# Shift blocks of a modulated norm divided over three engines, in a two-layer decoder trunk

## The chip, the core and the metric

The kernel runs on one core of one Trainium2 chip. The metric is the device time of one execution in microseconds (us). Each engine of the core takes its own instructions in order, and they signal one another by semaphores: TensorE (PE; its weight loads are PEld) multiplies matrices, VectorE (DVE), ScalarE (ACT) and GpSimd (POOL) work elementwise, and SyncE (SP) issues nearly all DMAs.

## The reference, cut to what matters

Layer 0 is attention and a SwiGLU, layer 1 a gated short convolution and a SwiGLU. Each of the four sub-layers begins with the same modulated norm:

```
S, D = 256, 1024                       # positions, features; x, c and all weights float32
sc = silu(c)
mod = sc @ w_ada[i] + b_ada[i]         # 6 * D columns: shift, scale, gate of both sub-layers
sh_m, sc_m, g_m, sh_f, sc_f, g_f = split(mod, 6)
h = x * rsqrt(mean(x * x) + EPS) * gain * (1 + sc_m) + sh_m
...
qkv = h @ w_qkv                        # layer 0
x = x + g_m * (attention(qkv) @ w_o)
h = modulate(x, norm_ffn, sh_f, sc_f)
x = x + g_f * swiglu(h, w_gate_up, w_down)
```

The change lies mostly in layer 0's first norm: its shift `sh_m` and scale `sc_m` are sums over 1024 inputs each, and the products for q and k cannot begin without them.

## The kernel before, in words

**Layout.** Everything is kept feature by position: `xT` is 128 x 8 x 256, eight blocks of 128 features (k = 0 to 7) by 256 positions. Every float32 product is done as three with operands split in a high and a low part: ACT copies the high part (`wh`, `m0h`), DVE subtracts it (`wl`, `m0l`), and `mm3` (L254, L255, L258) issues three matmuls. With weights on the left the second and third need `m0l` and `wl`.

**Stage 1, written out by hand (L554 to L629).** PE, DVE and ACT run exactly the order of the code. A prologue transposes x on PE (`turn_x`), sums its squares, and makes the row factors `rows0`. Then the loop runs over the eight feature blocks k: PE does block k's 36 matmuls into six accumulators (four `pq`, two `pk`), while the other engines make the operands of block n = k + 1:

- `scale_column` (L494): DVE sums the scale of block n over 1024 inputs (L109, one multiplication with a running sum) and turns it into one column (L492).
- `w_part` (L509): ACT copies and DVE subtracts the weights `wf_qk`, in three parts; the first before the norm's steps, two behind them.
- `normed` (L499): DVE multiplies the x block by its scale column and by `rows0`, into `t`.
- `h_operand` (L504): ACT adds the shift, into `m0h`; DVE makes `m0l` from `t`, the shift and `m0h`.
- The shift: `mod_sums` (L463) sums it on PE in the middle of block k's matmuls, ACT copies the result out (L473), `mod_columns` (L476) turns it to a column on PE, and ACT adds the bias (L487). For n = 1 this is one block; for n = 2, 4, 6 it covers blocks n and n + 1 together (256 columns wide).

`ja, jb` say behind which of the six accumulators the sums and the columns stand. `keep_warm` issues idle matmuls in the prologue. DVE is thus asked, for each block, for a sum, a column, a part of `wl`, `t`, `m0l`, and two parts of `wl`, in that order.

**Loads.** SP issues all loads in program order into five buffers of 1 MB (tag `wf`); a load waits until the buffer's last reader is done. A `wa_sh` buffer holds the shift matrices of two blocks, a `wa_sc` buffer the scale matrices of two.

**The rest** is ordered by a scheduler. `raw_gemm` (L414) begins the next three sub-layers: it multiplies weights by x before the norm is known, 12 matmuls per block k, and squeezes between them `norm.rstd()` (L347: PE sums the squares, ACT takes the root, DVE the reciprocal) in front of k = 2, and `norm.rows()` (L359: PE turns the result) in front of k = 4.

Of the kernel before, what the change touches and what calls it, by code (L numbers as in the profile page):

```python
# [30 lines left out]


@with_exitstack
def trunk_kernel(ctx: ExitStack, tc: tile.TileContext, x_t, cols_in, scale_in, shift_in, ada_in, qk_rows, kv_in, o_in,
                 in_in, out_in, gu_in, down_in, out_f):
    nc = tc.nc

    const = ctx.enter_context(tc.tile_pool(name="const", bufs=1))
# [375 lines left out]
    def raw_gemm(keys, norm, name):  # L414


        raw = norm.raw
        pss = [[psum.tile([P, S + 2], F32, tag=tag, name=f"raw_{name}_{i}{o}", bufs=n) for o in range(2)]
               for i, (tag, n) in enumerate((("gemm", 4), ("alt", 2)))]
        ws = [get(k) for k in keys]  # L420
        for k in range(KD):
            if k == 2:
                norm.rstd()
            if k == 4:
                rows = norm.rows()
                with tc.high_priority(400):
                    hs = modulated(norm.l, norm.sh, norm.scl, rows, name)
            for ps, (wh, wl) in zip(pss, ws):
                for o in range(2):
                    cs = slice(o * P, (o + 1) * P)  # L430
                    mm3(ps[o], (wh[:, k, cs], wl[:, k, cs]), (raw[0][:, k], raw[1][:, k]), k == 0, k == KD - 1)
        settle(name)
        res = []
        for i, tag in enumerate("sa"):
            y = tmp.tile([P, 2, S], F32, tag=tag, name=f"rawy_{name}_{i}")
            b = tmp.tile([P, 2], F32, tag="rawb", name=f"rawb_{name}_{i}")
            for o in range(2):
# [38 lines left out]
    def mod_columns(y, name):  # L476

        ps = ps_misc(f"mod_c_{name}")
        n = y.shape[1] // P
        for i in range(n):  # L480
            nc.tensor.matmul(ps[:, i:i + 1], y[:, i * P:(i + 1) * P], firsts, start=True, stop=True)
        return ps[:, :n]

    def shift_columns(y, k):
        ps = mod_columns(y, f"sh{k}")
        for n in range(ps.shape[1]):
            nc.scalar.activation(mcol(0, SH_M, k + n), ps[:, n:n + 1], AF.Identity,  # L487
                                 bias=b_cols[:, SH_M * KD + k + n:][:, :1])

    def scale_of(m, k, sums):  # L490

# [6 lines left out]

    def normed(k):  # L499
        t = tmp.tile([P, S], F32, tag="t", name=f"t_m0_{k}", bufs=3)  # L500
        nc.vector.scalar_tensor_tensor(t, xT[:, k], mcol(0, SC_M, k), rows0, op0=ALU.mult, op1=ALU.mult)
        return t

    def h_operand(k, t):  # L504
# [49 lines left out]
    with tc.manual_schedule(engines={mybir.EngineType.PE, mybir.EngineType.DVE, mybir.EngineType.Activation}):  # L554
# [30 lines left out]
        rr0 = rstd_rows(rstd0, "rr_0")  # L585
        rows0 = tmp.tile([P, S], F32, tag="rrow", name="rows0", bufs=1)
        nc.scalar.activation(rows0, rr0, AF.Copy)
        x_ps = turn_x(1, ps_alt)
        ps = mod_columns(y, "sc0")
        scale_of(mcol(0, SC_M, 0), 0, ps)  # L590
        y = mod_sums(shifts[:, 0:1], "sh0")
        t = normed(0)
        nc.vector.tensor_copy(xT[:, 2:4], x_ps)
        keep_warm(2)
        ops = w_operands(0, wf)
        shift_columns(y, 0)
        x_ps = [turn_x(i, ps_alt) for i in (2, 3)]
        operands(0, t, wf, ops)
        for i in range(2):
            nc.scalar.activation(xT[:, 4 + 2 * i:6 + 2 * i], x_ps[i], AF.Copy)  # L600
        keep_warm(4)
        for k in range(KD):
            n = k + 1
            if n < KD:
                if n % 2 == 0:
                    shifts, scales = ada_first(n // 2)
                    load_first(shifts, shift_in, n)
                    load_first(shifts, shift_in, n + 1)
                elif n == 1:
                    load_first(shifts, shift_in, 1)  # L610
                load_first(scales, scale_in, n)
                wf = first_rows(n)
            ja, jb = ((2, 3), (1, 2), (1, 4), (0, 3))[min(k, 3)]
            sums = n < KD and (n == 1 or n % 2 == 0)
            first_products(k, ops, range(0, ja))
            if sums:
                y = mod_sums(shifts[:, 1:2] if n == 1 else shifts, f"sh{n}")
            if n < KD:
                scale_column(scales[:, n % 2], n)
            first_products(k, ops, range(ja, jb))  # L620
# [202 lines left out]
def _lay_out(inputs):  # L823

    import numpy as np

    a = {k: np.asarray(v) for k, v in inputs.items()}

    def feats(v):
        return v.reshape(-1, P).T  # L830

    def chunks(w):

        k, j = w.shape[0] // P, w.shape[1] // CW
        return w.reshape(k, P, j, CW).transpose(2, 1, 0, 3).reshape(j, P, k * CW)

    ada = a["w_ada"].reshape(DEPTH, D, 6, KD, P)
    turned = ada.transpose(0, 2, 3, 4, 1)
    qkv = a["w_qkv"][0]

    def sums(part):

        return ada[0, :, part].reshape(KD, P, KD, P).transpose(2, 1, 0, 3).reshape(KD, P, D)

    return {
        "x_tok": a["x"][0].reshape(2, P, D).transpose(1, 0, 2),
        "cols": np.concatenate([feats(a[n]) for n in ("b_ada", "norm_mix", "norm_ffn", "conv_w", "q_gain", "k_gain", "c")],
                               axis=1),
        "scale": np.concatenate([sums(SC_M)[:1], turned[0, SC_M, 1:]]),
        "shift": sums(SH_M),  # L850
        "ada": turned.reshape(DEPTH, 6, 4, 2, P, D).transpose(0, 1, 2, 4, 3, 5).reshape(DEPTH, 6, 4, P, 2 * D),
        "qk_rows": qkv[:, :D + D // 2].reshape(KD, P, D + D // 2),
        "kv": chunks(qkv[:, D + D // 2:]),
        "o": chunks(a["w_o"][0]),
        "in": chunks(a["w_in"][0]),
        "out": chunks(a["w_out"][0]),
        "gate_up": np.stack([chunks(w) for w in a["w_gate_up"]]),
        "down": np.stack([chunks(w) for w in a["w_down"]]),
    }
# [21 lines left out]
```

## Time and profile before

| | us |
|---|---|
| median of 3 runs (lowest to highest) | 587.23 (586.2 to 587.33) |
| the profiled execution: its time, its span | 586.6, 584.8 |
| PE busy, share of the span | 577.4, 99% |
| DVE busy, ACT busy | 454.8 (78%), 316.1 (54%) |
| GpSimd busy | 1.1 |

The 1.8 us between the profiled time and its span lie before the first and after the last instruction. "Busy" counts a matmul from its start to its modelled end, and matmuls overlap, so short waits of PE do not show in that share: they are read from the starts of neighbouring matmuls, or from a wait that is named. Stage 1 reaches from the start to about 53 us.

### The profile page before, as it was taken

What the parts mean: (1) busy time and instruction counts of PE and PEld (TensorE: products, weight loads), DVE (VectorE), ACT (ScalarE), POOL (GpSimd) and SP (SyncE); (2) the same over time, 40 slices, a digit from 0 to 9 for tenths busy, and PEclk for the clock granted to TensorE, in tenths of its full rate; (3) what the DMA queues carried; (4) which work ended last, traced back from release to release, by engine and by line L of the source; (5) the groups of instructions that cost most, each with busy time, mean ns of one, the idle gap of its engine ahead of it and who ended that gap; (6) DMA issues with size and microseconds to landing.
All of it is one profiled execution on the core that took longest, in us unless ns stands there. A gap on an engine that the chain in (4) does not pass through costs nothing.

```text
span 584.8 us, 12020 instructions
## 1 busy us (share of the span) xinstructions
PE 577.4 (99%) x5032; PEld 569.8 (97%) x5032; DVE 454.8 (78%) x722; ACT 316.1 (54%) x526; POOL 1.1 (0%) x8
## 2 busy tenths in 40 slices
PE   7999999999999999999999999999999999999997
PEld 6899999999999999999999999999999999999997
DVE  4789989999999798967977999759986576555550
ACT  6457889597644454544445745446745345443330
POOL 0000000000000000000000000000000000000000
PEclk9999999999999999999999999999999999999999
DMA  8999999955898999968986379637387566655400
GB/s 316 396 380 409 356 331 334 341 208 187 335 377 303 347 334 342 331 240 303 330 310 254 129 291 366 247 122 261 128 331 280 180 261 216 238 174 200 148 19 18
DMA packets 25109, 156.04 MB, mean 267 GB/s; under 512 B 2784, under 2 KB 3168, under 8 KB 8928
## 3 DMA queue, kind: packets, MB, share of 16 engines
q1 hardware_dynamic: 25056, 155.28, 71.8%
q8 instruction: 39, 0.64, 0.4%
q14 instruction: 14, 0.11, 0.0%
HBM read 154.22 MB, written 1.05 MB: 266 GB/s over the span
## 4 chain that ended last, share of the span: by engine, by line
PE 93%; DMA 2%; DVE 2%; ACT 1%; issue 1%; SPq 0%; ACTq 0%; DVEq 0%
PE pu L255 7%; PE pu L254 7%; PE pu L258 7%; PE op_d L255 6%; PE op_d L254 6%; PE op_d L258 6%; PE pg L254 6%; PE pg L258 6%; PE pg L255 6%; PE raw_f L254 1%; PE op_o L258 1%; PE raw_f L255 1%; PE raw_f L258 1%; PE pb L258 1%; PE pb L254 1%; PE op_o L254 1%
## 5 line engine op out<-in xcount | busy, mean ns | idle before, releaser
L109 DVE SCALAR_TENSOR_TENSOR prod<-wa,c_all 128x1024 f32<-128x1024 f32 x80 | 97.6, 1220 | 18.0 <-DMA wa<-in_ada_dram 17.2
L98 ACT ACTIVATE wh_d<-wf_d 128x1024 fp32r<-128x1024 f32 (+1 forms) x48 | 45.2, 981 | 62.6 <-issue 41.9
L99 DVE TENSOR_TENSOR wl_d<-wf_d,wh_d 128x1024 fp32r<-128x1024 f32 (+1 forms) x48 | 52.8, 1132 | 23.9 <-ACT wh_d L98 23.7
L98 ACT ACTIVATE wh_g<-wf_g 128x1024 fp32r<-128x1024 f32 x44 | 45.7, 1053 | 44.6 <-issue 44.2
L98 ACT ACTIVATE wh_u<-wf_u 128x1024 fp32r<-128x1024 f32 x44 | 44.6, 1051 | 36.1 <-issue 30.5
L99 DVE TENSOR_TENSOR wl_u<-wf_u,wh_u 128x1024 fp32r<-128x1024 f32 x44 | 52.3, 1220 | 13.6 <-ACT wh_u L98 13.3
L99 DVE TENSOR_TENSOR wl_g<-wf_g,wh_g 128x1024 fp32r<-128x1024 f32 x44 | 53.5, 1219 | 2.4 <-ACT wh_g L98 2.2
L254 PE MATMUL op_d<-a0h,wh_d 128*128 128x256 f32 x176 | 48.6, 276 | 0.0
L258 PE MATMUL op_d<-a0h,wl_d 128*128 128x256 f32 x176 | 48.6, 276 | 0.0
L255 PE MATMUL op_d<-a1l,wh_d 128*128 128x256 f32 x176 | 48.6, 276 | 0.0
L254 PE MATMUL op_d<-a1h,wh_d 128*128 128x256 f32 x176 | 48.6, 276 | 0.0
L255 PE MATMUL op_d<-a0l,wh_d 128*128 128x256 f32 x176 | 48.6, 276 | 0.0
L258 PE MATMUL op_d<-a1h,wl_d 128*128 128x256 f32 x176 | 48.6, 276 | 0.0
L254 PE MATMUL pg<-f0h,wh_g 128*128 128x256 f32 x160 | 44.5, 278 | 0.0
L258 PE MATMUL pg<-f0h,wl_g 128*128 128x256 f32 (+3 forms) x164 | 44.5, 275 | 0.0
L254 PE MATMUL pg<-f1h,wh_g 128*128 128x256 f32 x160 | 44.3, 277 | 0.0
L255 PE MATMUL pg<-f0l,wh_g 128*128 128x256 f32 x160 | 44.2, 276 | 0.0
L254 PE MATMUL pu<-f0h,wh_u 128*128 128x256 f32 x160 | 44.2, 276 | 0.0
L258 PE MATMUL pg<-f1h,wl_g 128*128 128x256 f32 x160 | 44.2, 276 | 0.0
L258 PE MATMUL pu<-f1h,wl_u 128*128 128x256 f32 x160 | 44.2, 276 | 0.0
L255 PE MATMUL pu<-f0l,wh_u 128*128 128x256 f32 x160 | 44.2, 276 | 0.0
L255 PE MATMUL pg<-f1l,wh_g 128*128 128x256 f32 x160 | 44.2, 276 | 0.0
(294 smaller groups left out, 2022.8 us busy)
## 6 DMA issues: line engine op xcount, KB each, us to landing
wa<-in_ada_dram SPq DMA_DIRECT2D x40, 1024.0 KB, 6.8
wf_g<-in_gate_up_dram SPq DMA_DIRECT2D x22, 1024.0 KB, 5.3
wf_u<-in_gate_up_dram SPq DMA_DIRECT2D x22, 1024.0 KB, 4.9
wf_d<-in_down_dram SPq DMA_DIRECT2D x16, 1024.0 KB, 6.1
wf_d<-in_down_dram SPq DMA_DIRECT2D x8, 768.0 KB, 5.3
wa_sc<-in_scale_dram SPq DMA_DIRECT2D x8, 512.0 KB, 6.9
wa_sh<-in_shift_dram SPq DMA_DIRECT2D x8, 512.0 KB, 7.9
wf_qk<-in_qk_rows_dram SPq DMA_DIRECT2D x8, 512.0 KB, 6.7
```

The lines of the kernel that those rows point to most:

```text
L98: nc.scalar.activation(wh[:, a:b], wf[:, a:b], AF.Copy)
L99: nc.vector.tensor_sub(wl[:, a:b], wf[:, a:b], wh[:, a:b].bitcast(F32))
L109: nc.vector.scalar_tensor_tensor(t, w, 1.0, c_all, op0=ALU.mult, op1=ALU.mult, accum_out=dst)
L254: nc.tensor.matmul(ps, ah, bh, start=first, stop=False, skip_group_check=True)
L255: nc.tensor.matmul(ps, ah, bl, start=False, stop=False, skip_group_check=True)
L258: nc.tensor.matmul(ps[:, a:b], al, bh[:, a:b], start=False, stop=last, skip_group_check=True)
```

## The change

Four edits, in words: (1) The shift of odd blocks (n = 1, 3, 5, 7) is no longer summed on PE: its matrix is laid out like the scale's, DVE sums it with `ada_sum` (L109), ACT adds the bias. PE's sums for n = 2, 4, 6 become 128 columns wide instead of 256. (2) GpSimd multiplies x by `rows0`, blocks 1 to 7, into a new tensor `xn`; `normed` becomes an ACT multiplication of `xn` by the scale column. (3) In the prologue, block 0's shift sum goes in front of the transposes of the second pair of x blocks, and two `keep_warm` calls go. (4) `norm.rstd()` stands in front of k = 3 instead of k = 2. The array `out` (w_out, 4 MB) becomes the first argument, in front of x, and is not used earlier than before.

```diff
@@ -152 @@ (setup)
-    room("al", 1, "first_al")
+    xn = pair_rows(room("al", KD * S, "xn"))
@@ -419 @@ raw_gemm
-            if k == 2:
+            if k == 3:
                 norm.rstd()
@@ -481 @@
+    def shift_of(k, sums):
+        nc.scalar.activation(mcol(0, SH_M, k), sums, AF.Identity, bias=b_cols[:, SH_M * KD + k:][:, :1])
@@ -498 @@ normed
-        nc.vector.scalar_tensor_tensor(t, xT[:, k], mcol(0, SC_M, k), rows0, op0=ALU.mult, op1=ALU.mult)
+        if k == 0:
+            nc.vector.scalar_tensor_tensor(t, xT[:, k], mcol(0, SC_M, k), rows0, op0=ALU.mult, op1=ALU.mult)
+        else:
+            nc.scalar.activation(t, xn[:, k], AF.Copy, scale=mcol(0, SC_M, k))
@@ -585 @@ prologue
-        x_ps = turn_x(1, ps_alt)
         ps = mod_columns(y, "sc0")
         scale_of(mcol(0, SC_M, 0), 0, ps)
         y = mod_sums(shifts[:, 0:1], "sh0")
+        x_ps = turn_x(1, ps_alt)
         t = normed(0)
         nc.vector.tensor_copy(xT[:, 2:4], x_ps)
-        keep_warm(2)
...
-        keep_warm(4)
+        for k in range(1, KD):
+            nc.gpsimd.tensor_mul(xn[:, k], xT[:, k], rows0)
@@ -611 @@ loop over k
-            sums = n < KD and (n == 1 or n % 2 == 0)
+            sums = n < KD and n % 2 == 0
             first_products(k, ops, range(0, ja))
             if sums:
-                y = mod_sums(shifts[:, 1:2] if n == 1 else shifts, f"sh{n}")
+                y = mod_sums(shifts[:, 0:1], f"sh{n}")
             if n < KD:
+                if n % 2:
+                    ada_sum(mcol(0, SH_M, n), shifts[:, 1], f"sh{n}")
                 scale_column(scales[:, n % 2], n)
             first_products(k, ops, range(ja, jb))
             if n < KD:
                 ops_n = w_operands(n, wf)
                 if sums:
                     shift_columns(y, n)
+                else:
+                    shift_of(n, mcol(0, SH_M, n))
                 t = normed(n)
@@ -845 @@ _lay_out
-        "shift": sums(SH_M),
+        "shift": np.stack([turned[0, SH_M, k] if k % 2 else sums(SH_M)[k] for k in range(KD)]),
```

DVE's order in stage 1, before, for blocks n = 3 and n = 4 (`prod_sc` is the scale sum, `wl_qk_419` and `wl_qk_483` the two blocks' low weights):

```order
L109 SCALAR_TENSOR_TENSOR prod_sc_397,mod<-wa_sc_313,c_all 128x1024
L492 SCALAR_TENSOR_TENSOR mod<-mod,b_one,cols 128x1
L512 TENSOR_TENSOR wl_qk_419<-wf_qk_388,wh_qk_418 128x512
L501 SCALAR_TENSOR_TENSOR t_m_3_422<-xT,mod,rows_185 128x256
L506 SCALAR_TENSOR_TENSOR m0l<-t_m_3_422,mod,m0h 128x256
L512 TENSOR_TENSOR wl_qk_419<-wf_qk_388,wh_qk_418 128x512 x2
L109 SCALAR_TENSOR_TENSOR prod_sc_461,mod<-wa_sc_443,c_all 128x1024
L492 SCALAR_TENSOR_TENSOR mod<-mod,b_one,cols 128x1
L512 TENSOR_TENSOR wl_qk_483<-wf_qk_447,wh_qk_482 128x512
L501 SCALAR_TENSOR_TENSOR t_m_4_491<-xT,mod,rows_185 128x256
L506 SCALAR_TENSOR_TENSOR m0l<-t_m_4_491,mod,m0h 128x256
L512 TENSOR_TENSOR wl_qk_483<-wf_qk_447,wh_qk_482 128x512 x2
```

The same place of DVE's order after the change (`prod_sh` is the new shift sum):

```order
L109 SCALAR_TENSOR_TENSOR prod_sh_383,mod<-wa_sh_300,c_all 128x1024
L109 SCALAR_TENSOR_TENSOR prod_sc_385,mod<-wa_sc_301,c_all 128x1024
L492 SCALAR_TENSOR_TENSOR mod<-mod,b_one,cols 128x1
L516 TENSOR_TENSOR wl_qk_407<-wf_qk_374,wh_qk_406 128x512
L510 SCALAR_TENSOR_TENSOR m0l<-t_m_3_411,mod,m0h 128x256
L516 TENSOR_TENSOR wl_qk_407<-wf_qk_374,wh_qk_406 128x512 x2
L109 SCALAR_TENSOR_TENSOR prod_sc_450,mod<-wa_sc_432,c_all 128x1024
L492 SCALAR_TENSOR_TENSOR mod<-mod,b_one,cols 128x1
L516 TENSOR_TENSOR wl_qk_472<-wf_qk_436,wh_qk_471 128x512
L510 SCALAR_TENSOR_TENSOR m0l<-t_m_4_478,mod,m0h 128x256
L516 TENSOR_TENSOR wl_qk_472<-wf_qk_436,wh_qk_471 128x512 x2
```

The odd block has gained a sum of 1024 elements at its head, and both blocks have lost `t_m`.

ACT's order before, from block 3's first weight part to block 4's `m0h`:

```order
L511 ACTIVATE wh_qk_418<-wf_qk_388 128x512
L505 ACTIVATE m0h<-t_m_3_422,mod 128x256
L511 ACTIVATE wh_qk_418<-wf_qk_388 128x512 x2
L473 ACTIVATE mod_y_sh_459<-mod_ps_sh_450 128x256
L511 ACTIVATE wh_qk_482<-wf_qk_447 128x512
L487 ACTIVATE mod<-mod_c_sh_486,cols 128x1 x2
L505 ACTIVATE m0h<-t_m_4_491,mod 128x256
```

The same place after the change:

```order
L515 ACTIVATE wh_qk_406<-wf_qk_374 128x512
L485 ACTIVATE mod<-mod,cols 128x1
L505 ACTIVATE t_m_3_411<-xn,mod 128x256
L509 ACTIVATE m0h<-t_m_3_411,mod 128x256
L515 ACTIVATE wh_qk_406<-wf_qk_374 128x512 x2
L473 ACTIVATE mod_y_sh_448<-mod_ps_sh_439 128x128
L515 ACTIVATE wh_qk_471<-wf_qk_436 128x512
L485 ACTIVATE mod<-mod_c_sh_475,cols 128x1
L505 ACTIVATE t_m_4_478<-xn,mod 128x256
L509 ACTIVATE m0h<-t_m_4_478,mod 128x256
```

`t_m` now stands on ACT right in front of the `m0h` that reads it.

## Rows read from the trace of the kernel before

**Rows 1.** The page: span, and busy time of each engine.
```profile
span 584.8 us, 12020 instructions
...
PE 577.4 (99%) x5032; PEld 569.8 (97%) x5032; DVE 454.8 (78%) x722; ACT 316.1 (54%) x526; POOL 1.1 (0%) x8
```

**Rows 2.** Windows: length, busy (instructions) by engine, clock, DMA share, GB/s.
```profile
26.33:48.85 22.52, 22.52 (x209) 21.10 (x208) 18.99 (x38) 10.42 (x24) 0.00 (x0) 1.00 1.02 381
```

**Rows 3.** Timeline, DVE, block 3: start, duration, instruction, [idle before it <- releaser].
```profile
26.33 1.22 DVE L109 SCALAR_TENSOR_TENSOR prod_sc<-wa_sc,c_all 128x1024 f32<-128x1024 f32 x1
...
27.59 0.22 DVE L492 SCALAR_TENSOR_TENSOR mod<-mod,b_one,cols 128x1 f32<-128x1 f32 x1
27.73 0.68 DVE L512 TENSOR_TENSOR wl_qk<-wf_qk,wh_qk 128x512 fp32r<-128x512 f32 x1
28.33 0.48 DVE L501 SCALAR_TENSOR_TENSOR t_m<-xT,mod,rows 128x256 f32<-128x256 f32 x1
29.44 0.48 DVE L506 SCALAR_TENSOR_TENSOR m0l<-t_m,mod,m0h 128x256 fp32r<-128x256 f32 x1 [0.64 <-ACT m0h L505]
...
31.17 1.22 DVE L109 SCALAR_TENSOR_TENSOR prod_sc<-wa_sc,c_all 128x1024 f32<-128x1024 f32 x1
```

**Rows 4.** Timeline, ACT: block 3's m0h, and one shift column (block 1).
```profile
16.41 0.26 ACT L487 ACTIVATE mod<-mod_c_sh,cols 128x1 f32<-128x1 f32 x1
...
28.90 0.51 ACT L505 ACTIVATE m0h<-t_m,mod 128x256 fp32r<-128x256 f32 x1 [2.77 <-DVE t_m L501]
```

**Rows 5.** Timeline, block 2: ACT's first weight part, DVE's sum and m0l.
```profile
22.21 0.63 ACT L511 ACTIVATE wh_qk<-wf_qk 128x512 fp32r<-128x512 f32 x1 [0.93 <-DMA wf_qk<-in_qk_rows_dram]
...
20.93 1.23 DVE L109 SCALAR_TENSOR_TENSOR prod_sc<-wa_sc,c_all 128x1024 f32<-128x1024 f32 x1 [1.02 <-DMA wa_sc<-in_scale_dram]
...
24.60 0.48 DVE L506 SCALAR_TENSOR_TENSOR m0l<-t_m,mod,m0h 128x256 fp32r<-128x256 f32 x1 [0.64 <-ACT m0h L505]
```

**Rows 6.** Timeline, block 7: DVE's m0l, then PE's first two matmuls.
```profile
48.85 0.48 DVE L506 SCALAR_TENSOR_TENSOR m0l<-t_m,mod,m0h 128x256 fp32r<-128x256 f32 x1 [0.64 <-ACT m0h L505]
...
49.30 0.28 PE L254 MATMUL pq<-m0h,wh_qk 128*128 128x256 f32 x1
49.42 0.36 PE L255 MATMUL pq<-m0l,wh_qk 128*128 128x256 f32 x1
```

**Rows 7.** Timeline, PE: shift sums of 128 and 256 columns, and what follows each.
```profile
14.70 0.64 PE L469 MATMUL mod_ps_sh<-wa_sh,sc 128*32 128x128 f32 x16
15.28 0.39 PE L254 MATMUL pq<-m0h,wh_qk 128*128 128x256 f32 x1
...
29.41 1.07 PE L469 MATMUL mod_ps_sh<-wa_sh,sc 128*32 128x256 f32 x16
30.41 0.38 PE L254 MATMUL pq<-m0h,wh_qk 128*128 128x256 f32 x1
```

**Rows 8.** Timeline, DVE: two sums back to back, and block 1's first instruction.
```profile
61.94 1.23 DVE L109 SCALAR_TENSOR_TENSOR prod<-wa,c_all 128x1024 f32<-128x1024 f32 x1
...
63.21 1.22 DVE L109 SCALAR_TENSOR_TENSOR prod<-wa,c_all 128x1024 f32<-128x1024 f32 x1
...
14.42 1.23 DVE L109 SCALAR_TENSOR_TENSOR prod_sc<-wa_sc,c_all 128x1024 f32<-128x1024 f32 x1
```

**Rows 9.** Timeline, GpSimd: its largest instruction that reads a tile.
```profile
1.35 0.29 POOL L77 TENSOR_SCALAR_AFFINE_SELECT causal<-causal 128x128 f32<-128x128 f32 x1
```

**Rows 10.** Timeline, PE, layer 1's convolution: the sum of squares in raw_gemm.
```profile
312.79 0.28 PE L258 MATMUL raw_m<-zvh,wl_cu 128*128 128x258 f32 x1
313.47 0.27 PE L351 MATMUL ms_n<-inv_d,ss_n 128*128 128x1 f32 x1 [0.40 <-DVE ss_n L332]
```

**Rows 11.** Timeline, DVE and PE, last raw_gemm: low weights, and the turned rows.
```profile
404.96 1.20 DVE L99 TENSOR_TENSOR wl_g<-wf_g,wh_g 128x1024 fp32r<-128x1024 f32 x1
...
406.54 0.38 PE L300 MATMUL rr_n<-ident,rs_n 128*128 128x128 f32 x2
```

**Rows 12.** DMA, 0 to 12 us: GB/s in 40 slices of 0.3 us.
```profile
GB/s 0 0 0 0 0 26 175 171 164 273 314 137 137 68 178 273 382 410 410 396 437 437 410 396 437 423 410 437 410 382 417 423 437 416 410 423 423 410 437 382
```

More of the change, by code (lines that the diff above doesn't have):

```diff
@@ L33, in trunk_kernel @@
 @with_exitstack
-def trunk_kernel(ctx: ExitStack, tc: tile.TileContext, x_t, cols_in, scale_in, shift_in, ada_in, qk_rows, kv_in, o_in,
-                 in_in, out_in, gu_in, down_in, out_f):
+def trunk_kernel(ctx: ExitStack, tc: tile.TileContext, out_in, x_t, cols_in, scale_in, shift_in, ada_in, qk_rows, kv_in,
+                 o_in, in_in, gu_in, down_in, out_f):
     nc = tc.nc
@@ L482, in mod_columns @@
         return ps[:, :n]
+    def shift_of(k, sums):
+        nc.scalar.activation(mcol(0, SH_M, k), sums, AF.Identity, bias=b_cols[:, SH_M * KD + k:][:, :1])
     def shift_columns(y, k):
[L485 to L488, printed above, removed]
+        shift_of(k, mod_columns(y, f"sh{k}"))
     def scale_of(m, k, sums):
@@ L845, in _lay_out @@
     return {
+        "out": chunks(a["w_out"][0]),
         "x_tok": a["x"][0].reshape(2, P, D).transpose(1, 0, 2),
@@ L855, in _lay_out @@
         "in": chunks(a["w_in"][0]),
-        "out": chunks(a["w_out"][0]),
         "gate_up": np.stack([chunks(w) for w in a["w_gate_up"]]),
```

## The prediction

> **What bounds the kernel now.** I read the page first: PE is busy for 577.4 of 584.8 us [rows 1]. After stage 1 that is the bound, and this change hardly touches it, so the question is which engine ends stage 1. The windows come second: from 26.33 to 48.85 us, blocks 3 to 7, PE is busy all of the time and DVE for 18.99 of 22.52 [rows 2], so PE looks like the only candidate. The timeline of DVE, read third, says otherwise. One block starts its scale sum at 26.33 and the next at 31.17, a period of 4.84 us, and in it DVE waits once: 0.64 us, for ACT's `m0h` [rows 3]. It waits neither for a load nor for PE. DVE runs freely at 4.84 us per block. PE, meanwhile, alternates between blocks with and without a sum; it reaches block 7's second product at 49.42, 0.09 us after the `m0l` it needs has ended (48.85 + 0.48) [rows 6]. So PE and DVE are level: who becomes slower sets the end of the stage, and a saving on only one of them is lost.
>
> Block 2 has another start. DVE waits 1.02 us for the scale matrix, and ACT 0.93 us for the weights, which land at 22.2 [rows 5]. What is saved before that is waiting, not time.
>
> **The change, part by part, on the chain DVE - ACT - DVE.** In an even block DVE loses `t_m`, which ACT now does. From the sum's start the scale column is ready after 27.59 + 0.22 - 26.33 = 1.48 us; ACT follows DVE's `t_m` by 28.90 - 28.81 = 0.09; ACT's `t` I take at 0.51, as its `m0h` of the same size; ACT then reads its own result, for which the trace has no pair: nothing at least, 0.09 at most as between engines, and I take 0.05; `m0h` 0.51; `m0l` 0.03 behind it (29.41 to 29.44) [rows 3, 4]. That is 2.67 us to `m0l`, where it was 3.11. From `m0l` to the next sum stay 31.17 - 29.44 = 1.73. Even period: 4.40, a gain of 0.44. DVE does not get the whole of `t_m`'s place back: it still waits for ACT, now behind `wl`.
>
> In an odd block a sum comes on top. Two sums back to back start 63.21 - 61.94 = 1.27 us apart [rows 8]. Odd period: 5.67, a loss of 0.83.
>
> Block 1 (odd) starts at about 14.42 [rows 8] and ends at 14.42 + 5.67 = 20.09, still before the scale matrix of block 2 comes at 20.93: hidden, with 0.84 us left. Block 2: weights at 22.21, their first part 0.63, the shift column 0.26, then `t`, gap and `m0h` 1.07, and 0.03: `m0l` at 24.20 for 24.60, a gain of 0.40 [rows 4, 5]. From there the periods add up: block 3 24.20 + 5.67 = 29.87, block 4 34.27, block 5 39.94, block 6 44.34, block 7 50.01. Before it was 48.85 [rows 6]. All 36 products of block 7 need that `m0l`, so the stage ends **1.16 us later**.
>
> PE gives up the sum of block 1 (0.58 us from its start to the next product), and three times 1.00 - 0.58 = 0.42 [rows 7]: at least 1.84 us. It gains nothing: with 36 products 0.12 us apart [rows 6] its pair of blocks takes 2 x 4.3 + 0.58 = 9.2, DVE's 10.07. What hides this saving is DVE. If DVE were not in the way it would be worth all of its 1.84.
>
> `rstd` in front of k = 3: in the convolution PE's sum of squares starts 0.68 us behind the last product, where 0.12 is the pace; the 0.56 is a wait for DVE's last addition [rows 10]. Twelve products more (1.4 us) cover it: **-0.56 us**. The root and the reciprocal then have 1.4 us less. In the last of the three places the reciprocal now stands behind the second half of a `wl_g`, which ended at 404.96 + 1.20 = 406.16, and the turn was at 406.54 [rows 11]: I take nothing. If it is late it costs about 0.3 us there.
>
> Taken at nothing: block 0's shift earlier and the idle matmuls gone (both lie before block 2's landing, and six matmuls at 0.12 are 0.7 us); PE's new waits, up to 1.2 us in odd blocks, if the granted clock stays at the 1.00 of the window [rows 2]. SP's load of the scale matrices for blocks 4 and 6 now waits for a buffer that DVE frees; the DMA engines are fully busy there (share 1.02 [rows 2]), so the queue has a backlog that covers a later issue.
>
> GpSimd's seven multiplications: its nearest row is 0.29 us for 128 columns of one input [rows 9], so 0.58 for 256 and at most 1.16 with two inputs read one after the other. Even so ACT wants the first only at 14.42 + 1.27 + 1.48 = 17.2 us, and one more per block after that. Beside DVE I take them at nothing, which is the weakest entry; the other end is a rival.
>
> `out` in front of x moves the arrays in memory. In four slices of 0.3 us from 3.3 us on the loads run at 137, 137, 68 and 178 GB/s, later at about 410 [rows 12]. Those four moved what takes 0.38 us at 410, so 0.8 us is lost. A new place may give that back or lose it again: -0.8 to +0.8, taken as 0, since no row ties the slow slices to an address.
>
> **Sum:** +1.16 - 0.56 = +0.60 us. The profiled execution, 586.6, would become 587.2; it stands 0.63 below the median of 587.23. Against the median the forecast is **587.8 us**.
>
> **Rivals.**
> *GpSimd stands in DVE's way (slower).* Six of the seven multiplications fall between about 11 and 19 us, where DVE is doing blocks 0 and 1 on tensors read from the same SBUF. If each holds DVE for its own length, DVE loses 6 x 0.58 = 3.5 us; 0.84 is covered, as above, and the rest passes to the end: +2.6, or 590.4. It decides once the six together cost more than 0.84. For it: all of DVE's sums, `wl` and `m0l` read two SBUF tensors each [rows 3]. Against it: no row has GpSimd and DVE at work at once, and GpSimd may wait for DVE instead.
> The Trainium skill, "SBUF — State Buffer", section "Who interferes with whom", says just this: a VectorE instruction with two SBUF inputs and a GpSimd instruction that reads SBUF take turns on a shared read port, and the later one is blocked entirely. By that rule this rival is the forecast; no run here shows it yet.
> The same skill's "GPSIMD Engine Reference" times a two-input addition of 2048 float32 at 4497 ns, an estimated 0.56 us for 256, which would leave the rival's price about as it is.
>
> *PE sets the pace after all (faster).* If DVE's 0.64 us wait shrinks with ACT's new order, PE's saving arrives: -1.84 - 0.56 = -2.4, 584.8 us. For it: PE's unbroken busy time [rows 2]. Against it: DVE's period has no wait for PE to give back [rows 3].
>
> *The loads move with x.* All landings up to 22.2 shift by up to 0.8 us either way: 587.0 or 588.6.
>
> **How the numbers follow.** Forecast 0.42, GpSimd 0.27, PE 0.14, loads 0.17. About 0.2% (1.2 us) is what a measurement tells from no change: below 586.1 counts as faster, above 588.4 as slower. The forecast gives 0.34 same, 0.06 slower, 0.02 faster; GpSimd 0.25 slower, 0.02 same; PE 0.13 faster, 0.01 same; loads 0.10 same, 0.06 faster, 0.01 slower. Sum: faster 0.21, same 0.47, slower 0.32. The likeliest case alone spans 587.0 to 588.6; with the ends of the rivals 584.8 to 590.2 leaves out little more than the tails of GpSimd's price.
>
> **What would show it.** DVE's scale sums in stage 1 at alternating distances of 4.4 and 5.7 us; `m0l` of block 2 at about 24.2 and of block 7 at about 50.0; PE waiting about an `m0l` in each odd block; the sum of squares in the convolution without its wait. If DVE's instructions between 11 and 19 us grow longer or start late without a semaphore, it is GpSimd; if block 2's weights land well off 22.2, it is the loads; if block 7 starts before 48, my reading of DVE as the pace is wrong.

## The result and the profile after

The changed kernel took 591.08 us (median of 4 runs, 590.38 to 591.67) against 586.94 for the kernel before in the same comparison (586.2 to 587.33). The ratio is 1.0067, 95% interval [1.0045, 1.0088]: 4.1 us slower, above the range of 584.8 to 590.2. The profiled execution took 591.67 us.

The page of the kernel after, where [rows 1] stood for before:

```profile
span 589.9 us, 11981 instructions
...
PE 576.5 (98%) x5002; PEld 568.7 (96%) x5002; DVE 459.3 (78%) x723; ACT 319.0 (54%) x532; POOL 9.4 (2%) x15
```

PE has no more work, but the span is 5.1 us longer: PE waits. The windows of the kernel after, 10 us each (length, busy time with instructions of PE, PEld, DVE, ACT and GpSimd, granted clock, DMA share, GB/s), show where:

```profile
10.00:20.00 10.00, 7.33 (x68) 6.37 (x68) 9.10 (x12) 4.84 (x11) 8.10 (x7) 1.00 0.97 373
20.00:30.00 10.00, 8.40 (x66) 7.56 (x67) 7.47 (x13) 5.61 (x12) 0.25 (x1) 0.83 0.83 304
30.00:40.00 10.00, 10.00 (x98) 9.68 (x97) 8.58 (x17) 5.39 (x12) 0.00 (x0) 1.00 0.95 329
40.00:50.00 10.00, 9.67 (x87) 8.70 (x86) 8.08 (x17) 5.79 (x13) 0.00 (x0) 1.00 0.96 356
```

Two stretches stand out. From 10 to 20 us GpSimd is busy for 8.10 us, and DVE is at its fullest with only 12 instructions. From 20 to 30 us the clock is 0.83, where the kernel before had 1.00. The loads' share is 0.83 to 0.97, where it was 1.00 to 1.03 in the same four windows: their buffers come free later. From 5 to 50 us SP waits five times, 15.1 us in all, for DVE's `wl` before it issues shift and scale matrices; before the change it waited twice, 4.2 us.

GpSimd in the timeline of the kernel after (start, duration, instruction, count, idle time before it and releaser):

```profile
10.44 0.73 POOL L605 TENSOR_TENSOR xn<-xT,rows 128x256 f32<-128x256 f32 x1 [8.79 <-ACT rows L591]
12.63 7.61 POOL L605 TENSOR_TENSOR xn<-xT,rows 128x256 f32<-128x256 f32 x6 [1.46 <-DVE xT L597]
```

The first multiplication, which starts ahead of DVE's `t_m` of block 0, takes 0.73 us, inside the bounds of 0.58 to 1.16; the six that meet DVE at work take 7.61 / 6 = 1.27 each. DVE in the same stretch of the kernel after:

```profile
13.07 0.95 DVE L510 SCALAR_TENSOR_TENSOR m0l<-t_m,mod,m0h 128x256 fp32r<-128x256 f32 x1
13.95 2.36 DVE L516 TENSOR_TENSOR wl_qk<-wf_qk,wh_qk 128x512 fp32r<-128x512 f32 x2
16.23 1.76 DVE L109 SCALAR_TENSOR_TENSOR prod_sh<-wa_sh,c_all 128x1024 f32<-128x1024 f32 x1
...
18.03 1.63 DVE L109 SCALAR_TENSOR_TENSOR prod_sc<-wa_sc,c_all 128x1024 f32<-128x1024 f32 x1
...
19.71 0.56 DVE L492 SCALAR_TENSOR_TENSOR mod<-mod,b_one,cols 128x1 f32<-128x1 f32 x1
20.19 0.68 DVE L516 TENSOR_TENSOR wl_qk<-wf_qk,wh_qk 128x512 fp32r<-128x512 f32 x1
21.45 0.48 DVE L510 SCALAR_TENSOR_TENSOR m0l<-t_m,mod,m0h 128x256 fp32r<-128x256 f32 x1 [0.58 <-ACT m0h L509]
```

No instruction starts late behind a semaphore; the instructions themselves are longer. The `m0l` of 0.48 us takes 0.95, the sum of 1.23 [rows 3] takes 1.76 and 1.63, the column of 0.22 [rows 3] takes 0.56. As GpSimd ends, at 20.24, the durations are back: `wl` 0.68, `m0l` 0.48.

The three multiplications that meet DVE's two sums and the column, one by one:

```profile
15.72 1.19 POOL L605 TENSOR_TENSOR xn<-xT,rows 128x256 f32<-128x256 f32 x1
16.87 1.71 POOL L605 TENSOR_TENSOR xn<-xT,rows 128x256 f32<-128x256 f32 x1
18.54 1.71 POOL L605 TENSOR_TENSOR xn<-xT,rows 128x256 f32<-128x256 f32 x1
```

Their ends and those of DVE's instructions alternate: GpSimd 16.91, DVE 17.99, GpSimd 18.58, DVE 19.66, GpSimd 20.25. Each sum ends 1.08 us behind the multiplication that it met, each multiplication 0.59 behind the sum that it met. The two engines take turns: one instruction runs, the other stands until it is done.

What follows on PE of the kernel after:

```profile
18.16 0.28 PE L258 MATMUL pk<-wh_qk,m0l 128*128 128x256 f32 x1
21.47 0.38 PE L254 MATMUL pq<-m0h,wh_qk 128*128 128x256 f32 x1 [3.04 <-ACT m0h L509]
...
22.33 0.41 PE L254 MATMUL pq<-m0h,wh_qk 128*128 128x256 f32 x1
22.54 0.41 PE L255 MATMUL pq<-m0l,wh_qk 128*128 128x256 f32 x1
22.75 0.41 PE L258 MATMUL pq<-m0h,wl_qk 128*128 128x256 f32 x1
23.10 1.08 PE L469 MATMUL mod_ps_sh<-wa_sh,sc 128*32 128x128 f32 x16
24.11 0.58 PE L254 MATMUL pq<-m0h,wh_qk 128*128 128x256 f32 x1
```

PE waits 3.2 us for block 1's operands. Soon after it starts again, its matmuls come 0.21 us apart instead of 0.12 [rows 6], and the narrow sum takes 1.01 us where [rows 7] had 0.58: half speed, the 1.2 GHz level (the granted clock is 0.50 from 22.3 to 25.7 us). So PE's column for block 2's shift is late, and ACT waits for it:

```profile
25.96 0.26 ACT L485 ACTIVATE mod<-mod_c_sh,cols 128x1 f32<-128x1 f32 x1 [0.91 <-PE mod_c_sh L481]
```

DVE waits for ACT. The rows of `m0l` in the kernel after, blocks 2 to 7:

```profile
27.20 0.48 DVE L510 SCALAR_TENSOR_TENSOR m0l<-t_m,mod,m0h 128x256 fp32r<-128x256 f32 x1 [1.43 <-ACT m0h L509]
32.87 0.48 DVE L510 SCALAR_TENSOR_TENSOR m0l<-t_m,mod,m0h 128x256 fp32r<-128x256 f32 x1 [0.58 <-ACT m0h L509]
37.34 0.48 DVE L510 SCALAR_TENSOR_TENSOR m0l<-t_m,mod,m0h 128x256 fp32r<-128x256 f32 x1 [0.66 <-ACT m0h L509]
43.00 0.48 DVE L510 SCALAR_TENSOR_TENSOR m0l<-t_m,mod,m0h 128x256 fp32r<-128x256 f32 x1 [0.58 <-ACT m0h L509]
48.07 0.48 DVE L510 SCALAR_TENSOR_TENSOR m0l<-t_m,mod,m0h 128x256 fp32r<-128x256 f32 x1 [0.40 <-ACT m0h L509]
53.74 0.48 DVE L510 SCALAR_TENSOR_TENSOR m0l<-t_m,mod,m0h 128x256 fp32r<-128x256 f32 x1 [0.58 <-ACT m0h L509]
```

Odd blocks come 5.66 to 5.67 us behind even ones, as forecast (5.67). Block 7's `m0l` is at 53.74, where 50.01 was forecast and 48.85 was before [rows 6].

In the convolution the profiled execution of the kernel after still has PE's wait of [rows 10]:

```profile
319.44 0.28 PE L258 MATMUL raw_m<-zvh,wl_cu 128*128 128x258 f32 x1
320.07 0.61 PE L351 MATMUL ms_n<-inv_d,ss_n 128*128 128x1 f32 x4 [0.36 <-DVE ss_n L332]
```

The distance is 0.63 us, was 0.68. `rstd` is 12 products later, but so is DVE's last addition: it comes 4.3 us behind the first `raw_m` product, where it came 2.9 behind before.

### The profile page after: what moved, and what is told of

Its sections match the earlier page's. It is cut to its first block, busy times and chain, and to the rows that moved or that the text cites. A ratio compares the mean times of both kernels' runs of the same rounds, so it can differ in the third digit from the quotient of the medians.

```text
span 589.9 us, 11981 instructions
## 1 busy us (share of the span) xinstructions
PE 576.5 (98%) x5002; PEld 568.7 (96%) x5002; DVE 459.3 (78%) x723; ACT 319.0 (54%) x532; POOL 9.4 (2%) x15
## 4 chain that ended last, share of the span: by engine, by line
PE 62%; DVE 18%; DMA 14%; issue 5%; ACT 2%; SPq 0%; DVEq 0%; ACTq 0%
DMA wa<-in_ada_dram 11%; PE pu L258 4%; PE pu L254 4%; PE pu L255 4%; DVE prod L109 4%; PE op_d L254 3%; PE op_d L258 3%; PE op_d L255 3%; PE pg L258 3%; PE pg L254 3%; PE pg L255 3%; DVE wl_g L99 3%; DVE wl_d L99 2%; DVE wl_u L99 2%; PE raw_f L254 1%
## 5 line engine op out<-in xcount | busy, mean ns | idle before, releaser
L109 DVE SCALAR_TENSOR_TENSOR prod<-wa,c_all 128x1024 f32<-128x1024 f32 x80 | 97.8, 1223 | 23.8 <-DMA wa<-in_ada_dram 22.9
L258 PE MATMUL pu<-f0h,wl_u 128*128 128x256 f32 x160 | 44.2, 276 | 0.0
```

The costliest lines, as they stand in the source:

```text
L109: nc.vector.scalar_tensor_tensor(t, w, 1.0, c_all, op0=ALU.mult, op1=ALU.mult, accum_out=dst)
L258: nc.tensor.matmul(ps[:, a:b], al, bh[:, a:b], start=False, stop=last, skip_group_check=True)
```

## The experiments

"a" marks the kernel after with an edit, "b" the kernel before with one. The time of before was 586.8 us in each comparison (586.82, 586.80, 586.66, 586.86). The distances between one block's `m0l` and the next, read from DVE's timeline of each kernel, hold most of the readings (us). They are of one profiled execution each; the times are medians:

| kernel | block 0's m0l at | to 1 | 2 | 3 | 4 | 5 | 6 | 7 | time |
|---|---|---|---|---|---|---|---|---|---|
| before | 12.67 | 5.43 | 6.50 | 4.84 | 4.85 | 4.85 | 4.87 | 4.84 | 586.9 |
| after | 13.07 | 8.38 | 5.75 | 5.67 | 4.47 | 5.66 | 5.07 | 5.67 | 591.08 |
| a3_fill | 12.90 | 5.53 | 5.47 | 5.65 | 4.39 | 5.67 | 4.58 | 5.66 | 587.08 |
| a2_warm | 12.55 | 8.41 | 4.39 | 5.67 | 4.39 | 5.66 | 5.14 | 5.66 | 588.40 |
| a1_sums_on_pe | 13.01 | 6.72 | 5.05 | 4.40 | 6.30 | 4.40 | 5.59 | 4.39 | 588.11 |
| b1_gp_mul | 13.07 | 7.34 | 5.13 | 4.84 | 5.25 | 4.85 | 5.13 | 4.86 | 588.12 |
| b8_dve_late2 | 12.69 | 8.68 | 6.07 | 4.85 | 5.94 | 4.85 | 5.14 | 4.85 | 591.58 |
| b9_dve_late2_warm | 13.17 | 8.70 | 5.45 | 4.85 | 5.24 | 4.85 | 5.14 | 4.85 | 591.32 |

**b1_gp_mul and b2_gp_fill: GpSimd's work alone, read and write or write only.**

```diff
# before, in the prologue:
+        for k in range(1, KD):
+            nc.gpsimd.tensor_mul(xn[:, k], xT[:, k], rows0)   # b2: nc.gpsimd.memset(xn[:, k], 0.0)
```

> The kernel before, plus the seven GpSimd multiplications of x by the rows, whose result nothing reads. Theory 'GpSimd holds DVE': DVE's two-input instructions between about 12 and 19 us grow longer by 2 to 4 us in all, block 1's m0l moves from 18.1 to 20 or later, block 2's from 24.6 to 26 or later, and the total rises by 1.2 to 3 us. Rival 'the odd shift sums alone made the change slow': DVE's durations stay (0.48, 0.69, 1.23 us) and the total stays within 0.5 us.

> The kernel before, plus seven GpSimd fills of the same tiles with a constant: GpSimd is as present on the same tiles, but reads nothing. Theory 'it is GpSimd's reading that holds DVE' (the rule of the Trainium skill's page SBUF - State Buffer): DVE's durations and the total as before, within 0.5 us. Rival 'any GpSimd instruction in these microseconds delays DVE': DVE's instructions between 12 and 16 us grow as in the run with multiplications, total up by over 1 us.

b1: 588.12 us, ratio 1.0016 [0.9998, 1.0034]: the loss is not clear of noise in the time, but it is in the trace. DVE shows the same lengthening without any other part of the change:

```profile
13.65 2.37 DVE L512 TENSOR_TENSOR wl_qk<-wf_qk,wh_qk 128x512 fp32r<-128x512 f32 x2
15.94 1.75 DVE L109 SCALAR_TENSOR_TENSOR prod_sc<-wa_sc,c_all 128x1024 f32<-128x1024 f32 x1
...
18.83 0.94 DVE L501 SCALAR_TENSOR_TENSOR t_m<-xT,mod,rows 128x256 f32<-128x256 f32 x1
```

Block 1's `m0l` is at 20.41, as expected; block 2's at 25.54, earlier than the expected 26. PE waited 1.5 us here and its clock stayed at 1.00. b2: 587.21, ratio 1.0007 [0.9984, 1.0030]. It tells nothing of fills beside DVE, since they wait for nothing and ran from 1.58 to 3.40 us; b4_fill_late has them later.

**a1_sums_on_pe: the change without its odd sums on DVE.**

```diff
# after, in the loop:
-            sums = n < KD and n % 2 == 0
+            sums = n < KD and (n == 1 or n % 2 == 0)     # odd sums on PE, as before
```

> The changed kernel with the odd shift sums back on PE as in the kernel before (GpSimd's multiplications, ACT's t, the new prologue, rstd at k = 3 and the array order stay). Theory 'GpSimd first, odd sums second': blocks 0 and 1 still stretched, block 2's m0l at 25.5 to 26.5, then no 0.83 us per odd block; block 7's m0l at about 50 to 51 against 53.7, and the total 1.5 to 3 us above the kernel before. Rival 'the odd sums are all of it': total within 0.6 us of the kernel before.

588.11 us, ratio 1.0013 [0.9998, 1.0027]: 1.3 us above before, a little less than the 1.5 to 3 expected. GpSimd's cost is there (6.72 us to block 1, where 4.40 is the free period), and PE's waits in stage 1 stay short (0.7 us at most). Block 2's `m0l` came at 24.78, before the expected 25.5. The table shows 4.40 us in the odd blocks: DVE's own period without a second sum and without `t`, as forecast. In the even blocks ACT waits for PE's column (3.4 us in three waits), so PE sets the pace there.

**a2_warm: PE kept busy in its wait.**

```diff
# after, ahead of operands(n, ...) in the loop:
+            if k == 0:
+                keep_warm(28)
```

> The changed kernel with 28 idle matmuls on PE between block 0's and block 1's products, where PE waited 3.3 us for GpSimd-delayed operands and then ran at half its clock until 25.8 us. Theory 'the clock costs time through block 1': granted clock 1.00 from 20 to 30 us, block 2's shift column about 0.8 us earlier, m0l of block 2 at about 26.4 instead of 27.2, total 0.5 to 0.9 us below the changed kernel. Rival 'DVE paces and the clock is covered': m0l of block 7 and the total within 0.3 us of the changed kernel.

588.40 us, ratio to before 1.0022 [1.0006, 1.0037]: 2.7 us below the kernel after. The clock in 20 to 30 us is 1.00, and block 2 follows block 1 after 4.39 us instead of 5.75. The half clock had cost 1.36 us there. From DVE's 8.41 us in block 1 nothing is given back. The 2.7 us are more than the 0.5 to 0.9 expected; where the rest of them stands is said under what stays open.

**a3_fill: the changed order, with GpSimd writing only.**

```diff
# after:
-            nc.gpsimd.tensor_mul(xn[:, k], xT[:, k], rows0)
+            nc.gpsimd.memset(xn[:, k], 0.5)
```

> The changed kernel, but GpSimd fills xn with a constant instead of multiplying x by the row factors (the norm of blocks 1 to 7 is left out of the result); every other instruction stands as it does after the change. In the earlier run with fills GpSimd had done them before DVE's work of 10 us began. Theory (GpSimd's reads in DVE's way, and PE's wait with the half clock behind it, are the whole of the miss): DVE's instructions between 12 and 20 us take their old 0.48, 1.29, 1.23 us; m0l of block 1 at about 19.4 to 19.7, PE waits about 1.5 us there and keeps its clock; periods 4.4 and 5.67 us; block 7's m0l between 50.0 and 51.0 against 53.74; time 587.2 to 588.7. Rival (the order itself, the later rstd or the arrays cost the time): durations normal, but m0l of block 7 or the later stages still 2 us or more late, time 590 or more.

587.08 us, ratio 1.0004 [0.9986, 1.0021]. The whole 4 us is gone. The fills wait for nothing and ran from 1.59 to 3.42 us, so here nothing of GpSimd stands beside DVE's work at all. DVE of a3_fill, the same places as in the kernel after:

```profile
12.90 0.48 DVE L510 SCALAR_TENSOR_TENSOR m0l<-t_m,mod,m0h 128x256 fp32r<-128x256 f32 x1
13.30 1.29 DVE L516 TENSOR_TENSOR wl_qk<-wf_qk,wh_qk 128x512 fp32r<-128x512 f32 x2
14.50 1.22 DVE L109 SCALAR_TENSOR_TENSOR prod_sh<-wa_sh,c_all 128x1024 f32<-128x1024 f32 x1
...
15.76 1.23 DVE L109 SCALAR_TENSOR_TENSOR prod_sc<-wa_sc,c_all 128x1024 f32<-128x1024 f32 x1
...
49.85 0.48 DVE L510 SCALAR_TENSOR_TENSOR m0l<-t_m,mod,m0h 128x256 fp32r<-128x256 f32 x1 [0.58 <-ACT m0h L509]
```

Every duration is the old one, and block 7's `m0l` is at 49.85: the forecast's 50.01 to 0.16 us. In part that is luck: block 2's is 0.30 us earlier than forecast (23.90), and block 6's weights land late (4.58 where 4.40 was forecast). PE waits 0.8 us at block 1 and keeps its clock. The convolution's wait is gone as well:

```profile
314.69 0.28 PE L258 MATMUL raw_m<-zvh,wl_cu 128*128 128x258 f32 x1
314.81 0.50 PE L351 MATMUL ms_n<-inv_d,ss_n 128*128 128x1 f32 x4
```

So the forecast, 0.60 us above before, was right for a kernel whose GpSimd does not work beside DVE: a3_fill is 0.28 above, within the noise. That it is the reading, b4_fill_late and b5_gp_copy show.

**b4_fill_late and b5_gp_copy: what GpSimd must do to hinder DVE.**

```diff
# before; b4 (fills that wait for the row factors, so that they fall beside DVE):
+        nc.scalar.activation(xn[:, 1:KD, 0], rows0[:, 1:KD], AF.Copy)
+        for k in range(1, KD):
+            nc.gpsimd.memset(xn[:, k], 0.5)
# before; b5:
+        for k in range(1, KD):
+            nc.gpsimd.tensor_copy(xn[:, k], xT[:, k])
```

> The kernel before, plus one small ACT instruction that writes a column of a spare tensor from the row factors, and seven GpSimd fills of 128x256 behind it, so that they run at 11 to 17 us beside DVE; they write only (their result is not used). Theory (what DVE and GpSimd fight over is reading): DVE's durations stay at 0.48, 0.69, 1.29, 1.23 us while the fills run; block 7's m0l within 0.5 us of before (the ACT instruction costs up to 0.3), time 586.5 to 587.6. Rival (any GpSimd instruction lengthens DVE's): the scale sum of block 1 and the two wl take 1.6 us and 2.3 us or so as with the multiplications, block 7's m0l 1 us or more later, time about 588.

> The kernel before, plus seven GpSimd copies of an x block into a spare tensor (one input instead of two; the result is not used). They wait for x alone, so each runs as soon as its block of x is in place, from about 10 to 18 us. Theory (the cost goes by what GpSimd reads): a copy is shorter than a multiplication (0.3 to 0.6 us against 0.73), and DVE's instructions beside it grow by about half as much as beside the multiplications: DVE's total loss 1.0 to 1.7 us instead of 2.7 to 2.9, block 7's m0l 0.3 to 1.0 us later than before. Rival (a read port taken whole for each instruction): DVE loses as much as with two inputs, block 7's m0l 1.6 later. Rival 2 (only two-input instructions hinder): no loss.

b4: 586.97 us, ratio 1.0006 [0.9987, 1.0025]. Its GpSimd and DVE in 14 to 17 us:

```profile
14.39 1.23 DVE L109 SCALAR_TENSOR_TENSOR prod_sc<-wa_sc,c_all 128x1024 f32<-128x1024 f32 x1
...
14.77 1.83 POOL L604 MEMSET xn<- 128x256 f32 x7 [13.12 <-ACT xn L602]
...
16.33 0.69 DVE L512 TENSOR_TENSOR wl_qk<-wf_qk,wh_qk 128x512 fp32r<-128x512 f32 x1 [0.45 <-ACT wh_qk L511]
```

Seven fills beside most of a sum and the start of a `wl`, and neither is longer: writing does not hinder. b5: 586.70 us, ratio 0.9993 [0.9977, 1.0009]. Its four last copies and DVE beside them:

```profile
14.71 2.60 POOL L603 COPY xn<-xT 128x256 f32<-128x256 f32 x4 [1.17 <-ACT xT L600]
...
14.94 1.42 DVE L109 SCALAR_TENSOR_TENSOR prod_sc<-wa_sc,c_all 128x1024 f32<-128x1024 f32 x1
...
16.90 0.94 DVE L512 TENSOR_TENSOR wl_qk<-wf_qk,wh_qk 128x512 fp32r<-128x512 f32 x1 [0.28 <-ACT wh_qk L511]
```

Reading one input hinders, but less: the sum loses 0.19 us and the `wl` 0.25, with the first `m0l` (0.66) 0.62 in all, below the 1.0 to 1.7 of the theory. A copy holds DVE as a multiplication does: the `wl` ends 0.53 us behind the last copy (17.84 and 17.31), as the `wl` of the kernel after end 0.55 behind a multiplication. But a copy is shorter, 0.40 us, and only three of DVE's instructions were held by one. So the trace fits the mechanism of the first rival, in which each instruction takes its turn whole, and not its price. The slack ahead of block 2 covers the loss. The profiled execution of b5 took 588.19 us, its slowest; that does not touch these readings of stage 1.

**b3_rstd_out: the later rstd and the moved array alone.**

```diff
# before:
-            if k == 2:
+            if k == 3:
                 norm.rstd()
# and out_in ahead of x_t in the arguments
```

> The kernel before with two parts of the change only: rstd in front of k = 3, and the array of w_out as the first argument. Theory: in stage 1 nothing moves (block 7's m0l at 48.85 within 0.3), so the new place of the arrays is worth nothing; at the convolution the sum of squares no longer waits (gap 0.12 us instead of 0.68), and the later two places of rstd stay as they were: time 0.3 to 0.7 us below before, too little to be told in the time alone, but seen in the starts of PE's instructions there. Rival 1: the arrays move the loads: stage 1 0.5 us or more earlier or later. Rival 2: the gain at the convolution does not come, because the root and the reciprocal are then late: the next wait on PE behind k = 4 grows by about as much.

586.12 us, ratio 0.9984 [0.9966, 1.0001]. The sum of squares follows the last product without a wait:

```profile
313.81 0.28 PE L258 MATMUL raw_m<-zvh,wl_cu 128*128 128x258 f32 x1
313.92 0.50 PE L351 MATMUL ms_n<-inv_d,ss_n 128*128 128x1 f32 x4
```

The 0.56 us is real where DVE is on time, and rival 2 is out: no later wait of PE grew (`rr_n` follows its product after 0.12 us, as before). Block 7's `m0l` is at 48.51, within what versions with the arrays as before show (48.54 in b4, 49.13 in b2), so nothing here ties a gain or loss to the place of the arrays. This is the fastest version of the study, but its interval reaches 1: a gain is not shown.

**a4_no_gpsimd: the change without GpSimd, t on DVE as before.**

```diff
# after:
-            nc.scalar.activation(t, xn[:, k], AF.Copy, scale=mcol(0, SC_M, k))
+        nc.vector.scalar_tensor_tensor(t, xT[:, k], mcol(0, SC_M, k), rows0, op0=ALU.mult, op1=ALU.mult)  # all k
...
-        for k in range(1, KD):
-            nc.gpsimd.tensor_mul(xn[:, k], xT[:, k], rows0)
```

> The changed kernel without GpSimd's multiplications and without ACT's: t is made by DVE in one step again, as before; the odd shift sums stay on DVE. Theory (DVE is the pace; the multiplications were a gain for the period and a loss for 10 to 20 us): no instruction of DVE is lengthened, odd blocks take 4.84 + 1.27 = 6.11 us from sum to sum and even ones 4.84, m0l of block 1 at about 19.5, of block 2 at about 24.6, of block 7 at about 52.6, PE waits about 1 us in each block and keeps its clock; time about 589.5 to 590.5. Rival (PE is the pace and the narrower sums give time back): block 7's m0l at 51 or earlier, time 588.5 or less.

592.77 us, ratio 1.0092 [1.0056, 1.0128]: 2.3 us above what was expected. The interval overlaps that of the kernel after, so this does not show that it is slower than that one. Stage 1 went as expected up to block 6 (6.11 us in odd blocks); block 7's `m0l` came 6.52 behind, at 52.77, because the scheduler put a `wl_k` of 1.22 us in front of it. Behind stage 1 the scheduler ordered DVE and ACT otherwise than in the kernel after. The first `raw_f` product came at 134.23 us, 5.8 later than before, 1.9 more than that `m0l` was late; three waits of PE on the way (0.52, 0.27 and 0.20 us) are half of it, the rest was not followed up. GpSimd's `xn` has a value too: it takes 0.45 us off DVE's period (5.66 for 6.11, 4.39 for 4.85). In stage 1 it does not earn its cost: block 7's `m0l` is 0.97 us earlier here than in the kernel after.

**b6 to b9: the clock by itself.** DVE is made late in block 1 without GpSimd.

```diff
# before, ahead of scale_column (b6, b7: into a new tile of 128x3; b8, b9: into the scale's own column):
+                if n == 1:
+                    for i in range(3):
+                        ada_sum(mcol(0, SC_M, 1), scales[:, 1], f"extra{i}")
# b7, b9 also:
+            if k == 0:
+                keep_warm(32)
```

> The kernel before, with three sums of 1024 elements more on DVE in block 1 (into spare columns), and no GpSimd work: DVE is late there by 3 x 1.27 = 3.8 us without any contention, so that PE waits about 3.3 us at about 18 us, as in the changed kernel. Theory (PE's half clock follows from the length of its wait, whoever causes it): m0l of block 1 at 21.9, after the wait the granted clock is at about half until 25 to 26 us, ACT then waits for PE's shift column of block 2, and m0l of block 2 comes 0.6 to 1.2 us later than DVE's own 26.75: block 7's m0l at 51.6 to 52.3, time 589.6 to 590.6. Rival (the clock fell for another reason, GpSimd's work or the new order): clock 1.00 throughout 20 to 30 us, block 7's m0l at 51.0 or earlier, time 589.0 or less.

> The same with 32 idle matmuls on PE between the products of blocks 0 and 1, which fill most of the wait (each about 0.11 us, 3.4 us together). Theory: the granted clock stays at 1.00 from 20 to 30 us, m0l of block 2 at about 26.75 and of block 7 at about 51.0, time 0.6 to 1.5 us below the run without the idle matmuls. Rival (the clock is not what costs): no difference between the two, or this one is slower.

> The kernel before with three sums of 1024 elements more on DVE in block 1, as b6_dve_late, but written into the scale's own column ahead of the real sum, so that no tile is added. Theory (the half clock follows from PE's wait of about 3 us; the loss in the last sub-layer came from the new tile): clock about 0.83 in 20 to 30 us, m0l of block 7 3.5 to 4.2 us later than before's 48.85 (it was 52.67 in b6), the last sub-layer at 0.112 us per matmul again, time 589.8 to 591.0. Rival for the last sub-layer (the late stage 1 did it): time near 597 again.

> The same with 32 idle matmuls in PE's wait. Theory: clock 1.00 in 20 to 30 us; from m0l of block 0 to m0l of block 7 39.1 us as in b7 against 40.4 in b6; time 0.7 to 1.6 us below b8. Rival (the clock costs nothing that lasts): same time as b8 within 0.5 us or slower.

b6 took 597.67 and b7 598.5 us; the new tile spoiled their times (next experiment). b8 took 591.58, ratio 1.0081 [1.0067, 1.0095], and b9 591.32, ratio 1.0075 [1.0062, 1.0088]. PE of b8 at its wait:

```profile
18.29 0.28 PE L258 MATMUL pk<-wh_qk,m0l 128*128 128x256 f32 x1
21.39 0.38 PE L254 MATMUL pq<-m0h,wh_qk 128*128 128x256 f32 x1 [2.82 <-ACT m0h L505]
...
22.67 1.73 PE L469 MATMUL mod_ps_sh<-wa_sh,sc 128*32 128x256 f32 x16
```

The window 20 to 30 us of b8:

```profile
20.00:30.00 10.00, 8.48 (x62) 7.04 (x63) 7.49 (x14) 4.82 (x11) 0.00 (x0) 0.83 0.89 320
```

And of b9:

```profile
20.00:30.00 10.00, 10.00 (x94) 9.28 (x93) 8.10 (x15) 4.94 (x11) 0.00 (x0) 1.00 0.95 355
```

Behind a wait of 3.0 us the clock is at the same 0.83 with no GpSimd at work, and with idle matmuls in the wait it stays at 1.00. In stage 1 that is worth 0.62 us at block 2 and 0.70 at block 4 (table). The times do not differ, so the expectation of 0.7 to 1.6 us held for the stage and failed for the end. The two kernels differ in more than the clock, though: with the idle matmuls the scheduler ordered PE, DVE and ACT otherwise behind stage 1 (PE's first eight `q_sums` stand together in b8, at 57.83 us; in b9 they are two groups, at 57.08 and 58.07, with products of `wh_k` and `wl_k` between). By the traces b9's lead of 0.82 us at block 7's `m0l` is down to 0.12 when PE reaches `s<-qkT` (74.06 against 74.18 us). What comes later in b9's trace tells little of its median: the profiled execution took 594.43 us, 3.1 more, and has 2.6 us of waits of PE behind stage 1, where b8's has 0.6.

**b10_small_tile: a tile of 12 bytes more.**

```diff
# before, behind mod:
+    extra = const.tile([P, 3], F32, name="extra")
+    nc.gpsimd.memset(extra, 0.0)
```

> The kernel before with a tile of 128x3 float32 (12 bytes in a partition) behind mod in the pool of constants, filled once by GpSimd and never read: every later tile of the memory moves by its size. Theory (the place of the operands in SBUF sets the matmuls' pace in the last sub-layer): the last sub-layer at 0.116 us per matmul, time 593 to 594. Rival (the place does not matter): 586.5 to 587.5.

593.2 us, ratio 1.0105 [1.0092, 1.0118], as the theory has it. Stage 1 is that of before (block 7's `m0l` at 48.79). The last 160 us of the kernel before:

```profile
420.00:580.00 160.00, 160.00 (x1414) 160.00 (x1413) 93.11 (x104) 65.95 (x78) 0.00 (x0) 1.00 0.53 191
```

And of b10:

```profile
420.00:580.00 160.00, 160.00 (x1361) 160.00 (x1360) 92.63 (x102) 65.72 (x78) 0.00 (x0) 1.00 0.53 190
```

The same matmuls at the same granted clock, 53 fewer of them in the same time. b6 has the same 1361.

## Why the prediction was wrong

**The step that failed** is "Beside DVE I take them at nothing", of GpSimd's seven multiplications. DVE lost 8.38 - 5.53 = 2.85 us between the first two `m0l` against a3_fill, at the six multiplications that fall there: six of its instructions became 0.34 to 0.53 us longer. The rival that named this priced DVE's loss at 3.5 us and its passing on at 2.6, for a time of 590.4; it had the place and the mechanism right and lacked the clock. I gave it 0.27 because no row had both engines at work at once, which is no evidence against it. And the range ended at 590.2, below this rival's own 590.4: it left out the rival as I had priced it.

The Trainium skill, "SBUF — State Buffer", section "Who interferes with whom", states that a VectorE instruction with two SBUF inputs contends with a GpSimd instruction that reads SBUF and not with one that only writes, and that the one that comes later is blocked entirely. All of it is now seen here: 1.23 us became 1.75 beside multiplications and stayed 1.23 beside fills, and the ends of the two engines' instructions alternate, as the rows of GpSimd show. DVE still loses less than 0.73 us at each multiplication: one that had to stand ends 0.59 us behind the sum that held it, and the next sum ends 1.08 behind the multiplication, where it takes 1.23 by itself.

**The second failure** is the condition "if the granted clock stays at the 1.00 of the window". PE's wait at block 1 became 3.2 us instead of "up to 1.2", and the clock dropped behind it. Waits of 0.8 (a3_fill), 1.5 (b1) and 1.2 to 1.4 us (a4) left it at 1.00; 3.0 and 3.2 did not.

**The ledger at block 7's `m0l`**, after against a3_fill (53.74 - 49.85 = 3.89 us): prologue 0.17; GpSimd beside DVE 2.85; less 1.08, since a3_fill's block 2 waits for its scale matrix (0.62) and for ACT's first weight part (0.45; 5.47 us in all where the period is 4.39) and the kernel after would not; half clock 1.36; block 6 0.49, where the weights land later (ACT waits 2.13 us for them, 1.66 in a3_fill), and block 4 0.08. The sum is 3.87; the times differ by 4.00. The two profiled executions differ by more, 591.67 - 586.32 = 5.35: behind stage 1 that of the kernel after has waits of PE for `wl_d` (0.70) and `ss_n` (0.36) that a3_fill's has not. The waiting ahead of block 2 was taken at 0.84.

**What was right.** DVE sets the pace: 5.66 and 4.39 us per block (5.67 and 4.40 forecast). PE's shorter sums gave nothing back. All that is lost arrives at the end of the stage. The later `rstd` is worth its 0.56 us in b3_rstd_out and a3_fill; in the profiled execution of the kernel after it is not, since DVE reaches the convolution later relative to PE, which the prediction took as unchanged; a2_warm, with the same order, has the short distance of 0.12. That the new place of the arrays does nothing agrees with b3_rstd_out, to the 0.6 us by which such versions differ.

**Smaller slips.** The backlog of loads that was to cover SP's later issues did not cover them all: block 6 takes 4.58 us in a3_fill and 5.07 in the kernel after. And only a third of block 7's products read its `m0l`; the others but the first stand behind those in PE's order, so the conclusion holds.

**What stays open.** How much of the 4.1 us at the end is the clock's. In stage 1 filling the wait gives 1.36 us (a2_warm) and 1.3 (b9). At the end a2_warm gives 2.7 us and b9 nothing. a2_warm keeps the order of DVE and ACT, which b9 does not, so it is the better test of the two. By its trace 1.87 us stand at block 7's `m0l`, 0.52 of which are an earlier prologue; behind stage 1 it lacks the waits for `wl_d` and `ss_n` of the kernel after. Whether those belong to the clock or to that one execution is not shown.

## What to carry to other kernels

Work moved to GpSimd is not free because GpSimd is idle: where it reads SBUF beside VectorE instructions with two inputs, charge VectorE 0.3 to 0.5 us for each 128x256 multiplication that meets one of them, or let it fall where VectorE has slack. Where two engines are level, the delay of the one becomes a wait of the other, and here a wait of TensorE of 3 us was charged a second time through the clock. Before times of two versions are compared, look at the distance of the matmuls in a stage that neither touches, and at whether the scheduler kept the order of the rest.

## What the runs showed of the hardware that was not expected

- GpSimd is hindered as well as DVE: a multiplication took 0.73 us where it started ahead of DVE, 1.27 on average among DVE's two-input instructions. DVE's scale column on 128x1, with three small inputs, went from 0.22 to 0.56.
- With a tile of 12 bytes per partition that nothing reads, the matmuls of the last sub-layer went from 160 / 1414 = 0.113 us to 160 / 1361 = 0.118 at a granted clock of 1.00: 6.3 us of time. The stages before it were not touched. That it comes from the place of the tiles behind it is the likeliest reading, not shown; other sizes and single operands were not tried.
